# Local attention in a hybrid layer: the values of two chunks multiplied from one tile of weights, with new orders

## The chip, the cores and the metric

One core of one Trainium2 chip. The metric is the device time of one execution in microseconds; the kernel before has a median of 681.46 us over 3 runs (681.15 to 683.61). TensorE is called PE below, VectorE DVE, ScalarE ACT, GpSimd POOL; SP is the queue that issues nearly all DMAs, in its order.

## The reference

A decoder layer in float32 for 2048 tokens of width 1024. One input projection (1024 x 2816) feeds two groups of heads on the same normalised input: chunkwise retention (4 heads) and sliding-window attention (8 query heads, 2 key/value heads, head size 64, window 128). Each group's output is gated by SiLU, both are concatenated, projected back and added to `x`. The attention works in chunks of 128 tokens, each against its own and the preceding 128 keys:

```python
kband, vband = band(k), band(v)          # preceding chunk | this chunk: 256 keys
logits = jnp.einsum('bnqhgd,bnkhd->bhgnqk', qb, kband) * (SWA_HEAD_DIM ** -0.5)
mask = (dist[None] >= 0) & (dist[None] < WINDOW) & (key_pos >= 0)
logits = jnp.where(mask, logits + bias, NEG_INF)
probs = jax.nn.softmax(jnp.concatenate([logits, sink], axis=-1), axis=-1)[..., :-1]
out = jnp.einsum('bhgnqk,bnkhd->bnqhgd', probs, vband)
```

## The kernel before

**Products.** Both projections run as four stages of 2x2 block products with seven multiplications in place of eight (`products`): first 512 columns (attention's q, k, v and half of retention's v), then 384 (retention's q, k and the rest of v), then the gates (512), then the output projection (512). Each float32 operand is split by ACT and DVE into two parts (`split`), and a product is three passes over them. A stage is 7 multiplications x 8 pairs of chunks x 4 x 3 = 672 matmuls on the full array, the `acc<-w,x` of the profile.

**Everything else is fitted between the products.** `Program.emit` is a planner: every operation carries a cost, a due time counted in products and a tile share, and the planner writes one fixed order for each engine. `SHARE` caps the tiles of each use, `AHEAD` and `AHEAD_OF` how early loads may go, `LATER`, `CROWD`, `MOST`, `SOONER` weigh when small matmuls are gathered into one visit, `HELD` lists which intermediate tiles stay on chip instead of going out to DRAM and back, `TURNED` which are transposed by DMA, and `WIN`, `RET`, `GATE`, `LEAD` are due times of the attention, the retention and the gates. Once written, the order is fixed: each engine executes its instructions one after the other. On PE the tiled matmuls of attention and retention stand between runs of products.

**Attention** (`window`, `attend`, `values`). For chunk `c`, `attend` normalises q and k (`qn`, `kn`), turns k on PE (`ident,kn`) and q by DMA (`qT`), and multiplies the logits (`ks,qT`) in bands: each group of 32 queries `u` meets only the 160 keys from `32u` on. DVE adds the bias and takes the maximum, ACT takes the exponential into `lg` (128 x 640 for each key/value head), and a DVE block transpose of 32 x 32 turns `lg` into `pT`. `values` runs once for each pair of chunks. The tile `vn` holds values gathered so that row group `u` (32 partitions) has, in its block `b`, the 32 keys from `32u + 32b` on. The array works as eight tiles of 32 rows x 64 columns (four row groups, two heads). For each chunk of the pair, five blocks are multiplied with 128 columns of `pT` (4 query heads x 32 queries) and accumulated in PSUM; ACT copies the result out (`so`). Block 4 of the first chunk holds the same keys as block 0 of the second.

Tiles of 640 columns (`lg`, `pT`, `vn`) share one pool of nine; `vn` may use three of them.

**Retention** (`retention`) multiplies scores (`qkT`, `state,qkT`), outputs (`v,sT`) and state updates (`v,qk`) between products as well.

Of the kernel before, what the change touches and what calls it, by code (L numbers as in the profile page):

```python
# [29 lines left out]
F32 = mybir.dt.float32  # L30
# [9 lines left out]
P = 128  # L40
NCH = S // P
# [4 lines left out]
GRP = AH // KVH  # L46
# [8 lines left out]

NORMED = 4
SUMMED = 4
CAP = {"k": 84, "h": 6, "wide": 9, "bank": 8}
SMALL, COUNTS = 3, {"ms": 1, "rxt": 1, "rqk0t": 1, "rqk1t": 1}

SHARE = {"x": 18, "raw": 58, "acc": 55, "wr": 20, "wh": 20, "att": 54, "ret": 37, "rin": 49, "gate": 12, "mix": 28, "norm": 5, "res": 6, "turned": 7, "vn": 3, "first": 5, "block": 3, "rest": 6}

AHEAD_OF = {"x": 3.0, "wh": 8.0}

AHEAD, SPARE, SPARED = 13.5, 3, ("raw", "wr")

# [30 lines left out]

LATER, CROWD, MOST, SOONER = 0.0, -0.5, 4, 52.0
SETTLED, INSIDE = 0.8, 0.3


# [33 lines left out]
class Program:  # L139
# [5 lines left out]
    def op(self, cost, go, r=(), w=(), due=0.0, table=None, label="", also=(), many=0):  # L145


        o = Op()
        o.cost, o.go, o.due, o.after, o.set, o.label, o.many = cost, go, due, [], table, label, many * MORE
        o.n, o.left, o.ready, o.end, o.seen, o.by = len(self.ops), 0, 0.0, 0.0, 0.0, None  # L150
        deps = set()
        for b in r:
            if b.writer is not None:
                deps.add(b.writer)
        for b in w:
            if b.writer is not None:
                deps.add(b.writer)
            deps.update(b.readers)
        for b in r:
            b.readers.append(o)  # L160
        for b in w:
            b.writer, b.readers = o, []
        o.bufs = list(dict.fromkeys((*r, *w, *also)))
        for b in o.bufs:
            b.left += 1
        o.new = [b for b in (*w, *also) if b.ap is None and b.tag]
        for d in deps:
            if d is not o:
                d.after.append(o)
                o.left += 1  # L170
        self.ops.append(o)
        return o

    def emit(self):
# [28 lines left out]
        while done < count:  # L203
            best = None
            for e, found in avail.items():
# [4 lines left out]
                for due, n, o in found[:48]:  # L210
# [16 lines left out]
                    for b in o.new:  # L227
                        if b.ap is None:
                            need.setdefault(b.tag, []).append(b)
                    if any(due > now + AHEAD_OF.get(b.share, 1e9) for b in o.new):  # L230
                        continue
# [5 lines left out]
                    for tag, bs in need.items():  # L237
# [7 lines left out]
                        for share in {b.share for b in bs if b.share}:  # L245
                            many = used[share] + sum(b.share == share for b in bs)
                            if many > SHARE[share] - (spare if share in SPARED else 0):
                                short = True
# [90 lines left out]
TURN = (1.9635, 2.7, 1.35)  # L339


HELD = {"sums": ((5, 0), (5, 5), (6, 3), (7, 0), (7, 1), (7, 5), (7, 7)), "ro": (1, 9, 10, 12, 13, 14, 15), "q": (2, 3, 13, 14), "gates": (4, 6, 7), "so": (1, 2, 4, 9, 11)}

TURNED = {"q": range(NCH), "qk": range(NCH), "gated": (0, 2, 6, 8, 11, 13)}
EARLIER_Q, EARLIER_K = -1.0, 9.0
SCALED = (3.0, 2.1)


def dve(n, two=False, lat=0.08):
# [34 lines left out]
def dma(kb, issue=0.45):  # L387
    return {"Q": (0.0315 + kb / 320.95, 2.6, issue)}

VALUES = {"T": (2.28, 2.5, False)}


class Order:
# [27 lines left out]
def layer(ctx, tc, xt, xfirst, xtok, nw, w_in, w_rn, qkw, sinks, biasg, rope, decays, dmask, gpow, w_out, out):  # L423
    nc = tc.nc
    order = Order(tc)
    V, G, A, Q, T = (Engine(order, e) for e in (nc.vector, nc.gpsimd, nc.scalar, nc.sync, nc.tensor))
# [7 lines left out]
    def alloc(b):  # L434
        if b.tag == "bank":
            return psum.tile([P, 512], F32, tag=b.tag, bufs=CAP[b.tag], name=b.name)
        if b.tag in ("k", "h", "wide"):
            n = {"k": 512, "h": 256, "wide": 640}[b.tag]
            return sbuf.tile([P, n], b.dtype, tag=b.tag, bufs=CAP[b.tag], name=b.name)
        return little.tile(b.shape, F32, tag=b.tag, bufs=COUNTS.get(b.tag, SMALL), name=b.name)  # L440

    prog = Program(alloc, {"V": V, "G": G, "A": A, "Q": Q, "T": T})
    op = prog.op
# [5 lines left out]
        return Buf("h", None, F32, name)  # L449

    def wide(name, share=None):
        return Buf("wide", None, F32, name, share)

    def sb(name, shape):
        return Buf(name, shape, F32, name)
# [1 line left out]
    def ps(share="rest", name="m"):  # L457
        return Buf("bank", None, F32, name, share)
# [51 lines left out]
    wr = fixed([P, 4], "wr")  # L510
# [18 lines left out]
    akv_rows = dram.tile([(NCH + 1) * P, 512], F32, name="aq1_dram")  # L529
    akv_dram = {c: Buf(name="aq1_dram", ap=akv_rows[(c + 1) * P : (c + 2) * P, :]) for c in range(-1, NCH)}  # L530
# [139 lines left out]
    def blocks(src, base, seq, keep):  # L670
# [3 lines left out]
        for m, p in seq.all:  # L674
# [6 lines left out]
            elif m == 6:  # L681
# [7 lines left out]
                if keep:  # L689
                    for i, k in enumerate((5, 6, 7, 3)):  # L690
                        if (k, p) in HELD["sums"]:
                            sums[k, p] = held[k, p]
# [5 lines left out]
    sums = {}  # L698
# [50 lines left out]
    turn = Buf(name="turn", ap=())  # L749
# [154 lines left out]
    def retention(at):  # L904
# [18 lines left out]
        for c in range(NCH):  # L923
# [139 lines left out]

            ro = kb("ro", "mix" if c in HELD["ro"] else "ret")
            for i in range(2):
# [20 lines left out]
    def group_norm(st, ros, due):  # L1086
# [26 lines left out]
        for c, ro in ros:  # L1113
# [6 lines left out]
            op({"A": (1.55, 1.65, False)}, go, [ro, rg, nmu], [ro], due + 0.5, label="normalise")  # L1120
            if c in HELD["ro"]:
                held_ro[c] = ro
# [43 lines left out]
    def values(c, held, due):  # L1166


        tiles = []
        for k in range(2):  # L1170

            n = wide("vn", "vn")
            at = akv_rows[(c + k) * P : (c + k + 1) * P, 128:256]
            src = bass.AP(at.tensor, at.offset, [[512, P], [32 * 512, 5], [1, P]])
            op(
                dma(380, 0.6), lambda e, n=n, src=src: e.dma_start(n().rearrange("p (b d) -> p b d", d=P), src),
                [akv_dram[c + k - 1], akv_dram[c + k]], [n], due - 4, label="load vn",
            )
            tiles.append(n)
        pavs = [ps() for _ in range(4)]  # L1180

        def go(e):
            for k, n in enumerate(tiles):
                for b in range(5):
                    for u, q in enumerate(QUARTERS):
                        for g, r in enumerate((L, H)):
                            e.matmul(
                                pavs[u]()[r, k * P : (k + 1) * P].rearrange("p (i s) -> p i s", s=32),
                                n()[q, b * P + g * 64 : b * P + g * 64 + 64],
                                held[k][g]()[q, :].rearrange("p (i b s) -> p i b s", b=5, s=32)[:, :, b, :],  # L1190
                                start=(k == b == 0), stop=(b == 4), skip_group_check=True,
                            )

        op(VALUES, go, tiles + [t for h in held for t in h], pavs, due + 2, "bands", label="values", many=320)
        for k in range(2):
            so = kb("so", "mix" if c + k in HELD["so"] else "att")

            def go(e, so=so, k=k):
                for u in range(4):
                    e.activation(  # L1200
                        so().rearrange("p (i u s) -> p i u s", u=4, s=32)[:, :, u, :],
                        pavs[u]()[:, k * P : (k + 1) * P].rearrange("p (i s) -> p i s", s=32), AF.Copy,
                    )

            op({"A": (0.95, 1.05, False)}, go, pavs, [so], due + 2.1, label="so")
            if c + k in HELD["so"]:
                held_so[c + k] = so
            else:
                store(so_dram[c + k], so, due + 2.2)

    held_q, held_so, sums_of = {}, {}, []

    def qk_sums(p, row, col, b, due):

# [14 lines left out]
        if col == 1:  # L1229
# [4 lines left out]
            )  # L1234
        if col == 0 and c in HELD["q"]:
            held_q[c] = b
# [21 lines left out]
    L, H = slice(0, 64), slice(64, 128)  # L1258
    QUARTERS = [slice(i * 32, i * 32 + 32) for i in range(4)]

    def attend(c, a, b, fac, facs, due, bias_t, ks_t, nsnk):
        slot = c % 2
# [10 lines left out]
        if c in HELD["q"] and c in TURNED["q"]:  # L1273
# [16 lines left out]
            label="turn k", many=2,  # L1290
# [29 lines left out]
        lgs = [wide("lg") for _ in range(KVH)]  # L1320
# [15 lines left out]
        for bank, heads in enumerate([(2 * t + j, g) for j in range(2)] for t in range(2) for g in range(2)):  # L1336
            later, n = due + 0.5 + 0.2 * bank, len(heads)
            pl, g = pls[bank], heads[0][1]
            lg = lgs[g]
            out = Part(lg, lambda t, i=heads[0][0]: t[:, i * 160 : (i + 2) * 160])  # L1340

            part = lambda x, k=bank: x[:, c % SUMMED, k // 2 * 4 + k % 2 : k // 2 * 4 + 4 : 2]
# [4 lines left out]
            def go(e, pl=pl, out=out, heads=heads):  # L1347
# [9 lines left out]
                later, label="bias", also=(nm, lg),  # L1357
            )

            def go(e, out=out, heads=heads):  # L1360
# [9 lines left out]
                also=(nm, den, lg),  # L1370
            )
            weights_of[bank] = out
        pTs = []
        for g in range(KVH):
            lg, pT = lgs[g], wide("pT")
            op(
                {"V": (0.85, 0.95, False)}, lambda e, lg=lg, pT=pT: e.transpose(pT(), lg()), [weights_of[g], weights_of[2 + g]], [pT],
                due + 1.3 + 0.3 * g, label="turn weights", also=(lg,),
            )
            pTs.append(pT)  # L1380
        if c % SUMMED == SUMMED - 1:
# [97 lines left out]
    def go(e):  # L1479
# [10 lines left out]
        label="no values",  # L1490
# [28 lines left out]

WIN = (58.0, 4.8)
RET = (125.0, 2.1)
GATE = (145.0, 5.3)

LEAD = 12.0


_SHAPES = {
# [94 lines left out]
```

## Time and profile before

| | |
|---|---|
| median of 3 runs | 681.46 us (681.15 to 683.61) |
| span of the profiled execution | 679.0 us; the page gives no other time for it |
| PE busy | 672.1 us, 5812 matmuls |
| DVE busy | 594.3 us |
| ACT busy | 462.1 us |
| DMA | 162.63 MB |
| granted clock of PE | 1.000 |

The span runs from the first to the last instruction of the profiled execution. A row of the timeline has start, duration, engine, operation, output and inputs, shapes and count, and in brackets the idle time before it and what ended it. A row of waits has total, times and longest. Matmul ends are modelled, so distances from start to start are safer than durations. A float32 matmul of the program is two matmuls in the trace; a transpose, or a pass of a product, is one.

### The profile page before, as it was taken

The numbers are of one execution on the slowest core, as the hardware profiler recorded it, in microseconds if no ns is written. First come the engines' busy times: TensorE is split into PE (matmuls) and PEld (weight loads), VectorE is DVE, ScalarE is ACT, GpSimd is POOL, SyncE is SP. The second block draws the span as 40 slices with busy tenths as digits, with TensorE's granted clock in tenths as the row PEclk, the third lists the DMA queues.
The fourth block names the chain that finished last, engine by engine and source line by source line (L and its number), as shares of the span: only waits on it lengthen the run. The fifth ranks groups of instructions, "written<-read, shape, count | busy, mean of one in ns | idle before, by whom it ended". The sixth has DMA issues, their size and how long they took to land.

```text
span 679.0 us, 16052 instructions
## 1 busy us (share of the span) xinstructions
PE 672.1 (99%) x5812; PEld 571.4 (84%) x5812; DVE 594.3 (88%) x1369; ACT 462.1 (68%) x1121; POOL 15.6 (2%) x39
## 2 busy tenths in 40 slices
PE   9999999999999999999999999999999999999998
PEld 7888888889998999998878788888888888888886
DVE  6999967788897988999997998998889999997862
ACT  6763897758797776887977588987999844353300
POOL 0000000024100000000000000000000000000000
PEclk9999999999999999999999999999999999999999
DMA  9975698999969879999977879999998986055522
GB/s 314 383 237 217 202 372 291 297 305 296 273 182 248 243 225 280 301 279 319 234 207 246 220 223 288 214 331 253 260 247 219 267 192 199 1 170 171 181 99 94
DMA packets 155439, 162.63 MB, mean 240 GB/s; under 512 B 67808, under 2 KB 96352, under 8 KB 155360
## 3 DMA queue, kind: packets, MB, share of 16 engines
q1 hardware_dynamic: 155216, 161.61, 80.3%
q8 instruction: 46, 0.75, 0.5%
q14 instruction: 33, 0.27, 0.1%
q10 hardware_dynamic: 144, 0.00, 0.0%
HBM read 98.06 MB, written 49.35 MB: 217 GB/s over the span
## 4 chain that ended last, share of the span: by engine, by line
PE 94%; DVE 3%; DMA 2%; issue 1%; ACT 0%; SPq 0%; DVEq 0%; ACTq 0%
PE acc L419 82%; PE m L419 11%; DMA planes_dram<-apart 1%; DMA so_dram<-so 1%; DVE w L419 0%; DVE t L419 0%; DVE x L419 0%; DVE tsin L419 0%; DVE tcos L419 0%; DVE sT L419 0%; DVE state L419 0%; DVE qk L419 0%; ACT c L419 0%; ACT x L419 0%; ACT apart L419 0%
## 5 line engine op out<-in xcount | busy, mean ns | idle before, releaser
L419 PE MATMUL acc<-w,x 128*128 128x512 f32 (+1 forms) x2700 | 591.9, 378 | 0.2 <-PE m L419 0.2
L419 PEld LDWEIGHTS acc<-w,x 128*128 128x128 f32 x2700 | 492.1, 188 | 84.4 <-issue 4.3
L419 DVE TENSOR_TENSOR x<-x 128x512 fp32r<-128x512 f32 (+2 forms) x220 | 145.0, 685 | 17.4 <-ACT x L419 13.6
L419 ACT ACTIVATE x<-x 128x512 fp32r<-128x512 f32 (+1 forms) x187 | 111.8, 616 | 31.7 <-DVE x L419 13.9
L419 DVE TENSOR_TENSOR w<-w 128x512 fp32r<-128x512 f32 (+3 forms) x96 | 62.1, 671 | 3.3 <-ACT w L419 2.4
L419 ACT ACTIVATE lg<-lg,nm 128x160 f32<-128x160 f32 x128 | 53.0, 417 | 11.3 <-DVE nm L419 11.3
L419 DVE TENSOR_TENSOR s<-acc,s 128x512 f32<-128x512 f32 (+1 forms) x64 | 42.3, 660 | 14.5 <-PE acc L419 14.0
L419 DVE SCALAR_TENSOR_TENSOR w<-w,nw_sb 128x512 fp32r<-128x512 f32 (+3 forms) x72 | 49.6, 709 | 1.3 <-ACT w L419 1.3
L419 ACT ACTIVATE w<-w 128x512 fp32r<-128x512 f32 (+1 forms) x72 | 40.7, 603 | 12.8 <-PE acc L419 10.5
L419 DVE CUSTOM_DVE_ANT_0 lg<-m,bias,nsnk 128x160 f32<-128x160 f32 x128 | 40.6, 383 | 2.4 <-PE m L419 2.3
L419 DVE TENSOR_TENSOR t<-acc,t 128x512 f32<-128x512 f32 (+2 forms) x33 | 21.1, 641 | 15.0 <-PE acc L419 14.9
L419 ACT ACTIVATE s<-acc 128x512 f32<-128x512 f32 (+1 forms) x32 | 18.2, 569 | 17.3 <-PE acc L419 13.2
L419 ACT ACTIVATE w<-w,nw_sb 128x512 fp32r<-128x512 f32 (+3 forms) x43 | 27.6, 677 | 2.7 <-DMA w<-in_w_in 2.7
L419 DVE TENSOR_TENSOR r<-acc,t 128x512 f32<-128x512 f32 (+1 forms) x32 | 21.0, 655 | 9.1 <-PE acc L419 8.5
L419 ACT ACTIVATE x<-go 128x512 fp32r<-128x512 f32 x25 | 15.5, 626 | 17.6 <-PE acc L419 7.9
L419 ACT ACTIVATE ro<-ro,nmu,rg 128x128 f32<-128x128 f32 x64 | 25.1, 481 | 2.8 <-DVE nmu L419 2.8
L419 DVE STREAM_TRANSPOSE pT<-lg 128x640 f32<-128x640 f32 x32 | 25.7, 831 | 0.9 <-ACT lg L419 0.9
L419 DVE TENSOR_TENSOR t<-acc,s 128x512 f32<-128x512 f32 (+1 forms) x32 | 21.4, 667 | 4.8 <-PE acc L419 2.9
L419 ACT ACTIVATE apart<-qn 128x1024 uint16<-128x1024 uint16 x16 | 16.8, 1057 | 11.0 <-DVE qn L419 10.8
L419 ACT ACTIVATION_READ_ACCUMULATOR lg<-lg,nm 128x1 f32 x128 | 24.2, 189 | 0.0
L419 PE MATMUL m<-pT,vn 32*64 32x128 f32 x1280 | 21.2, 273 | 1.2 <-issue 0.8
L419 PE MATMUL m<-ks,qT 64*32 64x160 f32 x1024 | 22.1, 300 | 0.1
(144 smaller groups left out, 598.4 us busy)
## 6 DMA issues: line engine op xcount, KB each, us to landing
x<-in_xt SPq DMA_DIRECT2D x80, 256.0 KB, 4.7
planes_dram<-apart SPq DMA_DIRECT2D x54, 256.0 KB, 3.6
x<-s_dram SPq DMA_DIRECT2D x50, 256.0 KB, 4.3
w<-in_w_in SPq DMA_DIRECT2D x40, 256.0 KB, 5.1
xk<-in_xtok SPq DMA_DIRECT2D x32, 256.0 KB, 5.0
res<-in_xtok SPq DMA_DIRECT2D x32, 256.0 KB, 3.7
s_dram<-x SPq DMA_DIRECT2D x25, 256.0 KB, 3.9
vn<-aq_dram SPq DMA_DIRECT2D x16, 320.0 KB, 5.1
```

Source lines behind the costliest of these rows:

```text
L419: return lambda *a, **k: self.order.put(op(*a, **k))
```

## The change

Both chunks of a pair now use one `vn` of nine blocks (128 x 1152, 576 KB, one DMA). Block `b` below 4 is multiplied with the first chunk's columns, above 4 with the second's, and the shared block 4 once, with 256 columns that run over both chunks. For that, `pT` of both chunks of a pair lie in one tile of 1280 columns for each key/value head. The pool of nine becomes three pools: `lg` three tiles, `pT` two, `vn` one. The planner's cost for `values`, its instruction count (320 to 288) and its other settings are new, so all orders are planned anew.

```diff
-CAP = {"k": 84, "h": 6, "wide": 9, "bank": 8}
+CAP = {"k": 84, "h": 6, "lg": 3, "pT": 2, "vn": 1, "bank": 8}
-SHARE = {"x": 18, "raw": 58, "acc": 55, "wr": 20, "wh": 20, "att": 54, "ret": 37, "rin": 49, "gate": 12, "mix": 28, "norm": 5, "res": 6, "turned": 7, "vn": 3, "first": 5, "block": 3, "rest": 6}
-AHEAD_OF = {"x": 3.0, "wh": 8.0}
-AHEAD, SPARE, SPARED = 13.5, 3, ("raw", "wr")
+SHARE = {"x": 29, "raw": 58, "acc": 56, "wr": 22, "wh": 20, "att": 47, "ret": 22, "rin": 41, "gate": 9, "mix": 29, "norm": 7, "res": 24, "turned": 8, "vn": 3, "first": 5, "block": 3, "rest": 6}
+AHEAD_OF = {"x": 2.5, "wh": 6.5}
+AHEAD, SPARE, SPARED = 14.5, 4, ("raw", "wr")
-LATER, CROWD, MOST, SOONER = 0.0, -0.5, 4, 52.0
+LATER, CROWD, MOST, SOONER = 1.75, -1.0, 1, 32.0
-HELD = {"sums": ((5, 0), (5, 5), (6, 3), (7, 0), (7, 1), (7, 5), (7, 7)), "ro": (1, 9, 10, 12, 13, 14, 15), "q": (2, 3, 13, 14), "gates": (4, 6, 7), "so": (1, 2, 4, 9, 11)}
+HELD = {"sums": ((5, 0), (5, 5), (6, 4), (6, 6), (7, 1), (7, 2)), "ro": (1, 5, 8, 11, 12, 13, 15), "q": (3, 13, 14), "gates": (4, 5), "so": (0, 3, 6, 7, 11, 13)}
-TURNED = {"q": range(NCH), "qk": range(NCH), "gated": (0, 2, 6, 8, 11, 13)}
-EARLIER_Q, EARLIER_K = -1.0, 9.0
-SCALED = (3.0, 2.1)
+TURNED = {"q": range(NCH), "qk": range(NCH), "gated": (0, 2, 6, 7, 14, 15)}
+EARLIER_Q, EARLIER_K = 0.5, 9.0
+SCALED = (0.0, 2.35)
-VALUES = {"T": (2.28, 2.5, False)}
+VALUES = {"T": (2.05, 2.27, False)}
...
     def values(c, held, due):
-        tiles = []
-        for k in range(2):
-            n = wide("vn", "vn")
-            at = akv_rows[(c + k) * P : (c + k + 1) * P, 128:256]
-            src = bass.AP(at.tensor, at.offset, [[512, P], [32 * 512, 5], [1, P]])
...
-        pavs = [ps() for _ in range(4)]
+        n = wide("vn")
+        at = akv_rows[c * P : (c + 1) * P, 128:256]
+        src = bass.AP(at.tensor, at.offset, [[512, P], [32 * 512, 9], [1, P]])
...
+        pavs, pTs = [ps() for _ in range(4)], [t.whole for t in held[0]]
         def go(e):
-            for k, n in enumerate(tiles):
-                for b in range(5):
-                    for u, q in enumerate(QUARTERS):
-                        for g, r in enumerate((L, H)):
-                            e.matmul(
-                                pavs[u]()[r, k * P : (k + 1) * P].rearrange("p (i s) -> p i s", s=32),
-                                n()[q, b * P + g * 64 : b * P + g * 64 + 64],
-                                held[k][g]()[q, :].rearrange("p (i b s) -> p i b s", b=5, s=32)[:, :, b, :],
-                                start=(k == b == 0), stop=(b == 4), skip_group_check=True,
-                            )
-        op(VALUES, go, tiles + [t for h in held for t in h], pavs, due + 2, "bands", label="values", many=320)
+            for b in range(9):
+                for u, q in enumerate(QUARTERS):
+                    for g, r in enumerate((L, H)):
+                        t = pTs[g]()[q, :].rearrange("p (i b s) -> p i b s", b=5, s=32)
+                        k = b // 5
+                        if b == 4:
+                            x = t[:, 0:4, 4, :]
+                            part, x = pavs[u]()[r, 0 : 2 * P], bass.AP(x.tensor, x.offset, [x.ap[0], [512, 2], [160, GRP], [1, 32]])
+                            part = part.rearrange("p (k i s) -> p k i s", k=2, s=32)
+                        else:
+                            part, x = pavs[u]()[r, k * P : (k + 1) * P].rearrange("p (i s) -> p i s", s=32), t[:, 4 * k : 4 * k + 4, b - 4 * k, :]
+                        e.matmul(
+                            part, n()[q, b * P + g * 64 : b * P + g * 64 + 64], x, start=(b == 0), stop=(b in (4, 8)),
+                            skip_group_check=True,
+                        )
+        op(VALUES, go, [n, *(t for h in held for t in h)], pavs, due + 2, "bands", label="values", also=pTs, many=288)
...
-            lg, pT = lgs[g], wide("pT")
+            if slot == 0:
+                wholes[g] = wide("pT")
+            lg, pT = lgs[g], Part(wholes[g], lambda t: t[:, slot * 640 : slot * 640 + 640])
...
-WIN = (58.0, 4.8)
-RET = (125.0, 2.1)
-GATE = (145.0, 5.3)
-LEAD = 12.0
+WIN = (56.0, 4.8)
+RET = (124.5, 2.1)
+GATE = (143.0, 5.5)
+LEAD = 13.5
```

More of the change, by code (lines that the diff above doesn't have):

```diff
@@ L436, in alloc @@
             return psum.tile([P, 512], F32, tag=b.tag, bufs=CAP[b.tag], name=b.name)
-        if b.tag in ("k", "h", "wide"):
-            n = {"k": 512, "h": 256, "wide": 640}[b.tag]
+        if b.tag in ("k", "h", "lg", "pT", "vn"):
+            n = {"k": 512, "h": 256, "lg": 640, "pT": 1280, "vn": 1152}[b.tag]
             return sbuf.tile([P, n], b.dtype, tag=b.tag, bufs=CAP[b.tag], name=b.name)
@@ L451, in wide @@
     def wide(name, share=None):
-        return Buf("wide", None, F32, name, share)
+        return Buf(name, None, F32, name, share)
     def sb(name, shape):
@@ L1166, in values @@
     def values(c, held, due):
-        tiles = []
-        for k in range(2):
-            n = wide("vn", "vn")
-            at = akv_rows[(c + k) * P : (c + k + 1) * P, 128:256]
-            src = bass.AP(at.tensor, at.offset, [[512, P], [32 * 512, 5], [1, P]])
-            op(
-                dma(380, 0.6), lambda e, n=n, src=src: e.dma_start(n().rearrange("p (b d) -> p b d", d=P), src),
-                [akv_dram[c + k - 1], akv_dram[c + k]], [n], due - 4, label="load vn",
-            )
-            tiles.append(n)
@@ L1180, in values @@
-        pavs = [ps() for _ in range(4)]
-        def go(e):
-            for k, n in enumerate(tiles):
-                for b in range(5):
-                    for u, q in enumerate(QUARTERS):
-                        for g, r in enumerate((L, H)):
-                            e.matmul(
-                                pavs[u]()[r, k * P : (k + 1) * P].rearrange("p (i s) -> p i s", s=32),
-                                n()[q, b * P + g * 64 : b * P + g * 64 + 64],
-                                held[k][g]()[q, :].rearrange("p (i b s) -> p i b s", b=5, s=32)[:, :, b, :],
-                                start=(k == b == 0), stop=(b == 4), skip_group_check=True,
-                            )
@@ L1194, in values @@
-        op(VALUES, go, tiles + [t for h in held for t in h], pavs, due + 2, "bands", label="values", many=320)
+        n = wide("vn")
+        at = akv_rows[c * P : (c + 1) * P, 128:256]
+        src = bass.AP(at.tensor, at.offset, [[512, P], [32 * 512, 9], [1, P]])
+        op(
+            dma(580, 0.6), lambda e: e.dma_start(n().rearrange("p (b d) -> p b d", d=P), src),
+            [akv_dram[c + k] for k in (-1, 0, 1)], [n], due - 4, label="load vn",
+        )
+        pavs, pTs = [ps() for _ in range(4)], [t.whole for t in held[0]]
@@ new lines, in go @@
+        def go(e):
+            for b in range(9):
[12 more added lines that the diff above has]
+                            skip_group_check=True,
+                        )
@@ L1209, in values @@
                 store(so_dram[c + k], so, due + 2.2)
-    held_q, held_so, sums_of = {}, {}, []
+    held_q, held_so, sums_of, wholes = {}, {}, [], {}
     def qk_sums(p, row, col, b, due):
@@ L1374, in attend @@
         for g in range(KVH):
-            lg, pT = lgs[g], wide("pT")
+            if slot == 0:
+                wholes[g] = wide("pT")
+            lg, pT = lgs[g], Part(wholes[g], lambda t: t[:, slot * 640 : slot * 640 + 640])
             op(
                 {"V": (0.85, 0.95, False)}, lambda e, lg=lg, pT=pT: e.transpose(pT(), lg()), [weights_of[g], weights_of[2 + g]], [pT],
-                due + 1.3 + 0.3 * g, label="turn weights", also=(lg,),
+                due + 1.3 + 0.3 * g, label="turn weights", also=(lg, wholes[g]),
             )
```

## Prediction

> **What bounds the kernel now.** I read the page first, then the waits of TensorE (PE), the busy time by stretches, and PE's timeline around the bursts that the change touches.
>
> ```profile
> span 679.0 us, 16052 instructions
> PE 672.1 (99%) x5812; PEld 571.4 (84%) x5812; DVE 594.3 (88%) x1369; ACT 462.1 (68%) x1121; POOL 15.6 (2%) x39
> ...
> PE 94%; DVE 3%; DMA 2%; issue 1%; ACT 0%; SPq 0%; DVEq 0%; ACTq 0%
> ```
> ```profile
> PE m L419 <- DVE none L419: 1.2, 1, 1.2
> PE m L419 <- issue: 0.8, 1, 0.8
> PE m L419 <- ACT c L419: 0.5, 1, 0.5
> PE m L419 <- DVE state L419: 0.4, 1, 0.4
> PE m L419 <- DVE sT L419: 0.4, 1, 0.4
> ```
> ```profile
> 20.00:140.00 120.00, 120.00 (x531) 99.38 (x530) 105.69 (x195) 82.99 (x187) 0.00 (x0) 1.00 0.83 285
> ...
> 164.00:400.00 236.00, 233.87 (x3463) 207.42 (x3462) 212.55 (x601) 180.96 (x557) 6.97 (x13) 1.00 0.90 250
> 400.00:542.00 142.00, 141.58 (x1037) 117.58 (x1036) 131.78 (x329) 124.98 (x245) 0.00 (x0) 1.00 0.95 260
> ```
>
> PE is busy 672.1 of 679.0 us and carries 94% of the chain of waits. Its waits (second fence: total, times, longest) are 1.2 us at the start and 0.8 + 0.5 + 0.4 + 0.4 = 2.1 us in all that follows. The stretches give per engine busy time and count, then the granted clock (1.00 throughout) and the DMA share: in the attention and retention stages DVE is at 90 and 93%, DMA at 90 and 95%, both below PE. So the end is set by the amount and packing of PE's work. A change gains by taking work or mode changes off PE, and loses by making PE wait. The page gives the profiled execution no time beside its span. The 681.46 us median stands 2.5 us above the span, and I carry that difference over unchanged.
>
> **Part 1: the values burst.** Per pair of chunks, 160 hardware matmuls (80 calls, two each for float32) become 144 (72 calls). Eight tiles of 32 rows by 64 columns work at once.
>
> ```profile
> 186.23 4.43 PE L419 MATMUL acc<-w,x 128*128 128x384 f32 x24
> 190.59 1.34 PE L419 MATMUL m<-ks,qT 64*32 64x160 f32 x64
> 191.86 1.84 PE L419 MATMUL acc<-w,x 128*128 128x384 f32 x9
> 193.63 2.56 PE L419 MATMUL m<-pT,vn 32*64 32x128 f32 x160
> 196.12 4.96 PE L419 MATMUL acc<-w,x 128*128 128x384 f32 x27
> ...
> 204.99 7.56 PE L419 MATMUL acc<-w,x 128*128 128x384 f32 x42
> 212.48 2.09 PE L419 MATMUL m<-pT,vn 32*64 32x128 f32 x129
> 215.33 0.69 PE L419 MATMUL m<-pT,vn 32*64 32x128 f32 x31 [0.76 <-issue]
> 215.95 0.80 PE L419 MATMUL acc<-w,x 128*128 128x384 f32 x3
> ```
> ```profile
> 441.03 0.67 PE L419 MATMUL m<-qkT 64*64 64x128 f32 x16
> 441.52 0.62 PE L419 MATMUL m<-state,qkT 64*64 64x128 f32 x16
> 442.06 3.06 PE L419 MATMUL acc<-w,x 128*128 128x512 f32 x12
> ...
> 456.88 0.67 PE L419 MATMUL m<-qkT 64*64 64x128 f32 x16
> ...
> 457.80 0.62 PE L419 MATMUL m<-qkT 64*64 64x128 f32 x16
> ...
> 458.67 0.62 PE L419 MATMUL m<-qkT 64*64 64x128 f32 x16
> 459.11 0.62 PE L419 MATMUL m<-state,qkT 64*64 64x128 f32 x16
> 459.66 0.98 PE L419 MATMUL acc<-w,x 128*128 128x512 f32 x3
> ```
>
> I take times from start to next start, since the ends are modelled. An undisturbed values burst takes 196.12 - 193.63 = 2.49 us. What of that is streaming, the retention scores tell: three chunks take 459.66 - 456.88 = 2.78 us, one takes 442.06 - 441.03 = 1.03, so a chunk adds (2.78 - 1.03) / 2 = 0.875. It has 32 matmuls on four tiles, eight rounds, so one round of 128 float32 columns takes 0.109 us, and 1.03 - 0.875 = 0.155 is the cost of the mode. Values have 160 / 8 = 20 rounds: 2.19, with the mode 2.34. Of the 2.49 only 0.15 is neither.
>
> After the change a burst has 16 rounds of 128 columns and 2 of 256, which are again 20 rounds' worth: **the shared block is multiplied in fewer instructions, not in fewer columns.** So at most the 0.15 can go, if fewer instructions keep the tiles better fed. I take two thirds, 0.10 us, eight times: **-0.8 us**. The upper end is a burst that is bound by its instruction count: a tenth of 2.49, 0.25 each, -2.0. The lower end is below zero: the trace has no tiled matmul of 256 columns, and a long row could run slower than two short ones. The nearest rows:
>
> ```profile
> 1.18 3.78 PE L419 MATMUL m<-none 128*128 128x256 f32 x8 [1.18 <-DVE none L419]
> 4.86 2.53 PE L419 MATMUL acc<-w,x 128*128 128x512 f32 x7
> ```
>
> There eight float32 matmuls of 256 columns took 4.86 - 1.18 = 3.68 us, 0.46 each, against 2 x 0.109 = 0.218 here. At that pace two rounds would cost 2 x (0.46 - 0.218) = 0.48 more per burst, +3.9 us in all. I don't take it: they are the program's first matmuls, and the products' longer rows of 512 columns hold 120 / 531 = 0.226 us without any penalty. It stays in the range.
>
> [...]
>
> **Part 2: the order on PE.** Counted in the two built orders, PE leaves the full-array products for tiled matmuls 33 times before and 30 times after, and changes the tiling inside such a visit 7 times before and 10 after (half the logits now often stand directly behind the values). A visit costs 0.155 inside (above), and the run of products beside it also loses: 18 products more (42 against 24) take 7.49 - 4.36 = 3.13 us, 0.174 each, so the run of 24 lost 4.36 - 24 x 0.174 = 0.18 at its ends. Together 0.34. A change of tiling inside a visit spares the products, so I give it 0.155. Three visits fewer and three changes more: -1.02 + 0.47 = **-0.6 us** (between -1.0, if the change of tiling is free, and 0, if it costs like a visit). Products, logits, scores, updates, outputs and transposes are the same in number.
>
> **Part 3: what is moved or newly waits.** The 16 loads of 320 KB for `vn` become 8 of 576 KB; and the pools shrink to one `vn` tile, two `pT` tiles that hold both chunks, and three `lg`.
>
> ```profile
> vn<-aq_dram SPq DMA_DIRECT2D x16, 320.0 KB, 5.1
> ...
> q8 instruction: 46, 0.75, 0.5%
> ```
> ```profile
> SPq L419 <- PE acc L419: 54.4, 60, 5.8
> L419 DVE STREAM_TRANSPOSE pT<-lg 128x640 f32<-128x640 f32 x32 | 25.7, 831 | 0.9 <-ACT lg L419 0.9
> ```
>
> With one tile, the load for a pair can be issued only when the previous pair's matmuls are done. Bursts stand 212.48 - 193.63 = 18.9 us apart in the closest rows. The load, by size 576 / 320 x 5.1 = 9.2 us as an upper estimate, leaves 18.9 - 2.5 - 9.2 = 7 us: hidden, as long as SP gets to it. If not, PE waits in the burst and every product queued behind waits too. The two `pT` tiles are rewritten (0.83 us on DVE each) only after logits that stand behind the values on PE anyway: nothing. The new hand-picked lists move other traffic. Counted in the orders: five transfers of 256 KB more (query, gate and sum spills, less one output spill), eight `vn` loads fewer, so 0.77 MB more, 3.1 us at the 250 GB/s of the stretch 164 to 400. DMA is free there for 236 x 0.10 + 142 x 0.05 = 31 us over the two stretches, so it is covered; uncovered it costs those 3 us. DVE and ACT keep their numbers of operations.
>
> **Part 4: the stalls.** Three of the pauses in the trace:
>
> ```profile
> 354.94 0.46 PE L419 MATMUL m<-pT,vn 32*64 32x128 f32 x12
> 355.83 2.40 PE L419 MATMUL m<-pT,vn 32*64 32x128 f32 x148 [0.43 <-DVE state L419]
> ...
> 367.06 0.38 PE L419 MATMUL m<-qkT 64*64 64x128 f32 x2
> 367.93 0.55 PE L419 MATMUL m<-qkT 64*64 64x128 f32 x11 [0.50 <-ACT c L419]
> ```
>
> The burst at 212.48 took 215.95 - 212.48 = 3.47 us instead of 2.49, with a pause that waits for nothing shown ("issue"). I read it as instructions arriving late: queue 8 brought 46 pieces for PE's 2 x 5812 instructions, some 253 each, and a values burst alone is 320. [...] After the change a burst is 288, so such pauses get a little rarer, but where they fall depends on where a piece ends, which the new order moves everywhere. The new plan will have its own late operands too. I leave the 2.1 us of waits as they are: 0, between -2.1 and several us more.
>
> **Sum:** -0.8 - 0.6 + 0 + 0 = -1.4 us, 681.46 - 1.4 = **680.1 us**. A measurement of this kernel can tell some 0.5%, 3.4 us, from no change: below 678.05 is faster, above 684.87 slower.
>
> **Rivals.** *Instructions are the bound (faster).* If bursts are paced by instruction count, they give -2.0, the visits -0.6, and with thinner bursts and more lookahead (`AHEAD` 13.5 to 14.5, more `x` tiles) the 2.1 us of waits go: -4.7, 676.8 us. For it: the "issue" pause. Against it: the 109 ns rounds, and that all three must come together; the instructions and visits alone end at 678.9, inside "same". [...]
>
> *One `vn` tile holds up SP's queue (slower).* SP issues in order. Where the `vn` load waits for the values, the query turns, spills and the `x` loads of the next products wait behind it. SP's waits on products come to 54.4 us in 60, 0.9 each, and the longest is 5.8. If each of the seven loads that must wait delays the products by one such mean wait, 7 x 0.9 = 6.3: 680.1 + 6.3 = 686.4 us. It decides once SP is held longer than the loads behind it are early. For it: DMA at 90 to 95% leaves late loads little room to catch up. Against it: the 7 us of slack, and that PE barely waited with SP waiting this often.
>
> *The change does not shorten the burst at all* (only columns count): -0.6, 680.9 us, inside "same"; with slow 256-column rows 680.9 + 3.9 = 684.8, just inside it.
>
> **How the numbers follow.** Forecast with its neighbours inside 0.5% (also the burst unshortened): 0.47. Faster: 0.28, as removing mode changes and instructions is the sure part and the stalls that could go are there to see. Slower: 0.25, since late operands have no upper bound while the gain has one. The range runs from below the faster rival (676.8, less the bound of -1.0 for the visits in place of -0.6: 676.4) to the slower rival, 686.4; what lies outside is deep stalls above and a saving nobody in these rows explains below, at most 2 in 10.
>
> **What would show it.** Right: a values burst of 2.3 to 2.45 us from start to next start; 144 matmuls in it, 16 of them with 256 columns; PE above 98% busy; waits of PE after the start still 1 to 4 us; eight `vn` loads, none with PE waiting on it. Wrong towards faster: bursts near 2.25. Wrong towards slower: PE idle before `acc` or `m` with a DMA, `x` or `pT` named, longer SP waits on `m`, or bursts above 2.6 us without a pause in them.

## The result, and the profile after

The changed kernel is slower: 685.33 us (20 runs, 683.25 to 692.92) against 681.31 us (20 runs, 679.36 to 685.41), a ratio of 1.0076 with a 95% interval of 1.0058 to 1.0095. The forecast was 680.1 us and most likely no measurable change; the direction was wrong, and by the forecast's own bar of 684.87 the kernel is slower. The range held the time. The profiled execution took 684.4 us with a span of 682.6.

The page and the waits of PE of the changed kernel (total, times, longest):

```profile
span 682.6 us, 15825 instructions
PE 671.4 (98%) x5684; PEld 570.3 (84%) x5684; DVE 594.9 (87%) x1370; ACT 463.8 (68%) x1122; POOL 16.1 (2%) x39
PE 81%; DMA 6%; DVE 5%; ACT 5%; issue 2%; SPq 0%; ACTq 0%; DVEq 0%
```
```profile
PE m L419 <- issue: 1.5, 1, 1.5
PE acc L419 <- ACT s L419: 1.4, 1, 1.4
PE m L419 <- DVE s L419: 1.3, 1, 1.3
PE acc L419 <- DVE x L419: 1.2, 1, 1.2
PE m L419 <- DVE none L419: 1.2, 1, 1.2
PE m L419 <- DVE state L419: 0.5, 1, 0.5
PE m L419 <- DVE t L419: 0.4, 1, 0.4
PE m L419 <- DVE sT L419: 0.3, 1, 0.3
```

PE waits 6.6 us after the start where the kernel before waited 2.3 (all its rows summed; the prediction left out the smallest). Four waits of 1.2 to 1.5 us make up most of it, and PE's share of the chain falls from 94 to 81%. PE is also busy 0.7 us less than before (671.4 us), but its work did not become smaller. The 0.7 us lie in the first 12 us, shown here for the kernel before and the changed one:

```profile
4.86 7.53 PE L419 MATMUL acc<-w,x 128*128 128x512 f32 x29
4.79 7.58 PE L419 MATMUL acc<-w,x 128*128 128x512 f32 x32
```

The changed kernel starts three products more, 3 x 0.226 = 0.7 us: the first products of the kernel before stand some 0.43 us apart up to 6.3 us, those of the changed one 0.23 us almost at once. By the starts of single products, from the 41st product on (14.72 and 14.02 us) to PE's last matmul (675.79 and 679.27 us), less the waits, PE works 658.8 us before and 658.7 after. So the span's +3.6 us are the waits' +4.3 less the 0.7 of the start, and nothing is left over for the work.

The values bursts on PE's timeline, the first and the third:

```profile
188.01 2.53 PE L419 MATMUL m<-pT,vn 32*64 32x128 f32 x144
190.47 0.80 PE L419 MATMUL acc<-w,x 128*128 128x384 f32 x3
...
238.71 2.48 PE L419 MATMUL m<-pT,vn 32*64 32x128 f32 x138
242.64 0.44 PE L419 MATMUL m<-pT,vn 32*64 32x128 f32 x6 [1.45 <-issue]
243.01 0.78 PE L419 MATMUL m<-ks,qT 64*32 64x160 f32 x32
243.72 4.43 PE L419 MATMUL acc<-w,x 128*128 128x384 f32 x24
248.08 0.77 PE L419 MATMUL m<-ks,qT 64*32 64x160 f32 x32
248.79 1.50 PE L419 MATMUL acc<-w,x 128*128 128x384 f32 x7
```

An undisturbed burst takes 190.47 - 188.01 = 2.46 us, where the kernel before took 2.49 in its first burst and, by the starts of its single matmuls, 2.466 in others. Sixteen matmuls and sixteen weight loads fewer gained 5 ns. The third burst stands still 1.45 us for instructions. Half the logits directly behind it take 0.71 us (243.01 to 243.72).

Two of the late operands, on the timeline of ACT, DVE and PE:

```profile
162.57 0.49 ACT L419 ACTIVATE s<-acc 128x384 f32<-128x384 f32 x1 [1.73 <-DMA aq_dram<-t]
163.12 1.14 PE L419 MATMUL acc<-w,x 128*128 128x384 f32 x5 [1.38 <-ACT s L419]
...
348.09 0.37 DVE L419 CUSTOM_DVE_ANT_0 lg<-m,bias,nsnk 128x160 f32<-128x160 f32 x1
348.40 0.37 DVE L419 CUSTOM_DVE_ANT_0 lg<-m,bias,nsnk 128x160 f32<-128x160 f32 x1
348.70 0.68 DVE L419 TENSOR_TENSOR x<-x 128x512 fp32r<-128x512 f32 x1
349.43 0.73 PE L419 MATMUL acc<-w,x 128*128 128x512 f32 x2 [1.21 <-DVE x L419]
```

At 163.1 a product waits for the copy of its PSUM bank, and that copy waits for an output transfer (`aq_dram<-t`) to land. At 349.4 a product waits for its `x`, which stands on DVE behind the biases of a chunk's logits. Neither has to do with the values burst; both are places in the new order.

### The profile page after: what moved, and what is told of

It is laid out like the page before. It is cut to its first block, busy times and chain, and to the rows that moved or that the text cites. A ratio compares the mean times of both kernels' runs of the same rounds, so it can differ in the third digit from the quotient of the medians.

```text
span 682.6 us, 15825 instructions
## 1 busy us (share of the span) xinstructions
PE 671.4 (98%) x5684; PEld 570.3 (84%) x5684; DVE 594.9 (87%) x1370; ACT 463.8 (68%) x1122; POOL 16.1 (2%) x39
## 4 chain that ended last, share of the span: by engine, by line
PE 81%; DMA 6%; DVE 5%; ACT 5%; issue 2%; SPq 0%; ACTq 0%; DVEq 0%
PE acc L419 71%; PE m L419 11%; DMA aq_dram<-t 2%; DMA planes_dram<-apart 2%; DMA w<-in_w_in 1%; DVE x L419 1%; ACT x L419 1%; ACT sq L419 1%; DVE s L419 1%; ACT apart L419 1%; ACT qk L419 1%; DVE w L419 1%; DMA aq_dram<-r 1%; ACT lg L419 0%; SPq L419 0%
## 5 line engine op out<-in xcount | busy, mean ns | idle before, releaser
L419 ACT ACTIVATE so<-m 128x128 f32<-128x128 f32 x64 | 11.9, 294 | 17.2 <-PE m L419 10.2
L419 PE MATMUL m<-pT,vn 32*64 32x128 f32 (+1 forms) x1152 | 21.1, 285 | 1.5 <-issue 1.5
```

The lines of the kernel that those rows point to most:

```text
L419: return lambda *a, **k: self.order.put(op(*a, **k))
```

## The experiments

**Columns or instructions: the burst by itself.** First, the orders of the changed kernel left as they are, with the shared block multiplied twice with 128 columns again.

```diff
-            for b in range(9):
+            for b, k in [(b, 0) for b in range(5)] + [(b, 1) for b in range(4, 9)]:
...
```

> The changed kernel with its orders on every engine unchanged, but the shared block multiplied twice with 128 columns again (160 matmuls per burst for 144). Theory A (columns set the burst, orders set the loss): the burst stays at 2.46 to 2.47 us from start to next start, and the time stays with the changed kernel's, 685.3 us give or take 1.5. Rival B (instructions set the burst): 16 matmuls more cost 0.25 us per burst, 2.71, and 687.3 us. Rival C (the rows of 256 columns or their addressing are what made it slower): the 4 us come back, 681.3.

Then with the second half of the shared block left out.

```diff
                         if b == 4:
                             x = t[:, 0:4, 4, :]
-                            part, x = pavs[u]()[r, 0 : 2 * P], bass.AP(x.tensor, x.offset, [x.ap[0], [512, 2], [160, GRP], [1, 32]])
-                            part = part.rearrange("p (k i s) -> p k i s", k=2, s=32)
+                            part = pavs[u]()[r, 0:P].rearrange("p (i s) -> p i s", s=32)
```

> The changed kernel with the second half of the shared block left out: block 4 is multiplied with the first chunk's 128 columns alone, 144 matmuls per burst as before and two half rounds fewer. Theory A (columns set the burst): 2.46 - 2 x 0.109 = 2.24 us from start to next start. Rival B (instructions set the burst): 2.46 as in the changed kernel.

PE's timeline, first of the doubled block, then of the halved one:

```profile
291.01 2.54 PE L419 MATMUL m<-pT,vn 32*64 32x128 f32 x160
293.48 0.75 PE L419 MATMUL m<-ks,qT 64*32 64x160 f32 x26
297.13 0.47 PE L419 MATMUL m<-ks,qT 64*32 64x160 f32 x6 [2.90 <-issue]
297.53 6.52 PE L419 MATMUL acc<-w,x 128*128 128x384 f32 x27
```
```profile
269.67 2.32 PE L419 MATMUL m<-pT,vn 32*64 32x128 f32 x144
271.92 0.77 PE L419 MATMUL m<-ks,qT 64*32 64x160 f32 x32
```

With 160 matmuls the burst takes 293.48 - 291.01 = 2.47 us, with 144 and two half rounds less 271.92 - 269.67 = 2.25: 0.21 less than the changed kernel's 2.46, near the expected 2 x 0.109. **The burst is set by its columns.** The one time of the halved kernel, 685.88 us, tells nothing beyond that: its waits are 8.7 us.

The time of the doubled block was a miss for every theory: 694.45 us (ratio 1.016, 1.0112 to 1.0209), though the order on every engine is the same. Its trace names the reason in the fence above: pauses for instructions, 7.2 us in three on the matmuls `m` alone. PE's instructions come in packets of queue 8, a piece of 256 in each: in the traces of the kernel before and of the changed one 11504 and 11247 of them (matmuls, weight loads and semaphore instructions) start between the first packet and the last, 255.6 for each packet. With 256 more on PE (16081 instructions in all against 15825) the page counts 46 packets in place of 45, and the pieces end at other places of the same order; that three ends now fall on dense bursts is the author's reading of the three pauses. And a pause costs more than itself: the busy time by stretches around the pause at 294 to 297 (after the engines' busy times: granted clock, DMA share and rate; the third row is a part of the second),

```profile
294.00:297.40 3.40, 0.50 (x16) 0.14 (x5) 0.51 (x1) 1.44 (x7) 0.00 (x0) 1.00 0.96 255
297.40:303.00 5.60, 5.60 (x28) 5.47 (x23) 3.46 (x12) 4.94 (x14) 0.00 (x0) 0.70 0.40 143
298.10:301.50 3.40, 3.40 (x13) 3.40 (x12) 2.00 (x8) 3.40 (x12) 0.00 (x0) 0.50 0.44 157
303.00:309.00 6.00, 6.00 (x65) 5.46 (x63) 6.00 (x18) 3.11 (x11) 0.00 (x0) 1.00 0.83 250
```

shows the granted clock at 0.50 for 3.4 us behind it, in which the products start 0.32 us apart in place of 0.17. The trace has such stretches at three places, 13.7 us in all, which at half the clock cost up to 6.8 us. With the waits' 5.5 us over the changed kernel's they cover the span's 10.3. The pause is 2.90 us by the row; other runs show the same behind shorter ones (last section).

**Code or settings.** First the new values code and its pools with the settings of the kernel before (`SHARE`, `AHEAD_OF`, `AHEAD`, `LATER`, `HELD`, `TURNED`, `EARLIER_Q`, `SCALED`, `VALUES`, `WIN`, `RET`, `GATE`, `LEAD` and what stands on their lines), some of them here against the changed kernel:

```diff
-AHEAD, SPARE, SPARED = 14.5, 4, ("raw", "wr")
+AHEAD, SPARE, SPARED = 13.5, 3, ("raw", "wr")
...
-LATER, CROWD, MOST, SOONER = 1.75, -1.0, 1, 32.0
+LATER, CROWD, MOST, SOONER = 0.0, -0.5, 4, 52.0
...
-WIN = (56.0, 4.8)
-RET = (124.5, 2.1)
-GATE = (143.0, 5.5)
+WIN = (58.0, 4.8)
+RET = (125.0, 2.1)
+GATE = (145.0, 5.3)
```

> The new values code and the new pools (lg three, pT two, vn one) with all of the planner's settings of the kernel before (tile shares, lookahead, held tiles, due times) and its cost for values. Theory A (the new settings' orders bring late operands): waits of PE back near 3 us, 680 to 683 us. Rival C (the values code or its small pools cost the time): 684 to 687 us. Rival D (any new order is a draw, whatever the settings): anything from 679 to 690, with stalls at new places.

Then the reverse: the kernel before, its code and pools untouched, with those settings of the changed kernel, except that `VALUES` stays at 2.28.

```diff
-AHEAD, SPARE, SPARED = 13.5, 3, ("raw", "wr")
+AHEAD, SPARE, SPARED = 14.5, 4, ("raw", "wr")
...
-WIN = (58.0, 4.8)
-RET = (125.0, 2.1)
-GATE = (145.0, 5.3)
+WIN = (56.0, 4.8)
+RET = (124.5, 2.1)
+GATE = (143.0, 5.5)
```

> The values code and the pool of the kernel before, with all of the planner's settings of the changed kernel. Theory A (the new settings' orders bring late operands): 684 to 687 us. Rival C (the values code or its small pools cost the time): 680 to 682 us. Rival D (any new order is a draw): anything from 679 to 690, and the stalls not at the places where the changed kernel has them.

Measured: 698.68 us (1.0249, 1.0202 to 1.0296) and 691.62 us (1.0129, 1.0093 to 1.0165). Both halves of the change by themselves are slower than the whole. That fits neither A nor C, and both times lie above D's range (679 to 690) too. What is left is D's mechanism, worse than expected: new orders stall at new places. That settings and code belong together, because the settings were picked for the order they give, is the reading that the runs below test. Among PE's waits with the old settings

```profile
PE acc L419 <- ACT w L419: 4.6, 2, 3.3
PE acc L419 <- DVE w L419: 3.7, 2, 1.9
PE m L419 <- DVE sT L419: 2.8, 3, 1.4
```

the first two are weights, which the changed kernel never waited for.

**Instructions that arrive late.** The orders untouched, only the stream of PE's instructions shifted at the start: most warming matmuls are replaced by many of one column, 23 in the changed kernel (shown) and 34 in the kernel before.

```diff
-        for _ in range(WARM):
+        for _ in range(2):
             e.matmul(pw()[:, 0:256], none()[:, 0:P], none()[:, 0:256], start=True, stop=True)
+        for _ in range(23):
+            e.matmul(pw()[0:1, 256:257], none()[:, 0:1], none()[:, 0:1], start=True, stop=True)
```

> The changed kernel with its orders unchanged; only its instructions on TensorE stand 84 places later (two of the four warm-up calls at the start give way to 23 multiplications of one column), so that its pieces of 256 instructions end at other places. Theory A (pauses in a burst are instructions arriving late, the other long waits are late operands): the pause of 1.6 us in the burst at 238.7 is gone, the waits on ACT s (1.4), DVE x (1.2), DVE s (1.3) stay at their places, and the time falls by 1 to 2 us to 683 to 684.5. Rival (the pause is a late operand or a bank that the profile doesn't show): it stays, 685.3. Should a pause come up at another burst instead, A holds too, but without a gain.

> The kernel before with its orders unchanged and its instructions on TensorE 128 places later (two warm-up calls give way to 34 multiplications of one column). [...] Rival (where the pieces end doesn't matter): 681.3.

PE's timeline in the changed kernel shifted, at the third burst, and in the kernel before shifted:

```profile
243.97 2.53 PE L419 MATMUL m<-pT,vn 32*64 32x128 f32 x144
246.43 0.78 PE L419 MATMUL m<-ks,qT 64*32 64x160 f32 x32
```
```profile
266.52 2.27 PE L419 MATMUL m<-pT,vn 32*64 32x128 f32 x139
271.79 0.66 PE L419 MATMUL m<-pT,vn 32*64 32x128 f32 x21 [3.00 <-issue]
272.37 0.33 PE L419 MATMUL m<-ident,kn 128*128 128x128 f32 x1
```

In the first the pause is gone (246.43 - 243.97 = 2.46), and in the second a burst without a pause before got one of 3.00 us: 688.28 us (1.0114, 1.0081 to 1.0147), 7.0 us above the 681.3 expected should it not matter where the pieces end. (Of the 2.3 us of waits in the kernel before, one of 0.8 was for instructions.)

But the edit does a second thing: it takes away half of the warming. The first 12 us of the kernel before shifted and of the changed kernel shifted:

```profile
4.96 7.25 PE L419 MATMUL acc<-w,x 128*128 128x512 f32 x20
4.62 7.61 PE L419 MATMUL acc<-w,x 128*128 128x512 f32 x21
```

They start 20 products where the kernel before starts 29, and 21 for the changed kernel's 32. At the 41st product that is 1.85 and 2.35 us lost. So of the 7.4 us of span that the kernel before lost by the shift, some 5.5 are left for the places where the pieces end: pauses for instructions of 5.7 us in place of 0.8, and a stretch at half the clock behind the longest. The pieces themselves are packets of queue 8 in the traces. In all 14 pauses above 0.3 us that the traces of these runs put down to "issue", PE goes on 1.2 to 1.6 us after such a packet has landed (at 270.21 and 271.79 us for the pause of 3.00). That instructions arrive late is shown.

The changed kernel came to 684.41 us (1.0066, 1.0028 to 1.0105); the expected gain of 1 to 2 us over 685.33 cannot be told from none. Its start lost 2.35 us, and the wait on `ACT s` takes 2.88 us in place of 1.38, with the granted clock at 0.50 for 3.4 us behind it. Not all late operands stayed either: the wait on `DVE x` takes 0.5, that on `DVE s` is gone, and one of 1.4 on `DVE state` before a product is new. So these waits change with the time at which PE comes to them, at an unchanged order.

**A draw, or the planner's cost.** `VALUES` tells the planner what a burst costs. The change lowered it by a tenth with the instruction count, from 2.28 to 2.05; the burst stayed the same, so the new plan counts on 0.23 us per burst that never came. Four kernels try this. The kernel before with one due time moved by 0.1:

```diff
-WIN = (58.0, 4.8)
+WIN = (58.1, 4.8)
```

> The kernel before with one due time of the attention moved by 0.1 (WIN 58.0 to 58.1), and the orders planned anew from it. Theory D (any new order is a draw, and the kernel before is a good one): 683 to 692 us, with stalls of TensorE above 1.5 us at places where the kernel before has none. Rival (orders from nearly the same settings run nearly alike): 680 to 682.5.

The changed kernel with the cost put back:

```diff
-VALUES = {"T": (2.05, 2.27, False)}
+VALUES = {"T": (2.28, 2.5, False)}
```

> The changed kernel with the planner's cost for the values put back to that of the kernel before (2.28 for 2.05), which is what a burst of 2.46 us corresponds to, and planned anew. Theory E (the planner was misled by a cost that is 0.23 us too small per burst): operand waits shrink, 681 to 683.5. Theory D (any new order is a draw, and the settings were picked for the order that they gave): 684 to 695.

The changed kernel with the due time moved, and then with both edits:

```diff
-WIN = (56.0, 4.8)
+WIN = (56.1, 4.8)
```

> The changed kernel with one due time of the attention moved by 0.1 (WIN 56.0 to 56.1), planned anew. Theory D (an order picked with its settings, and any new one is a draw): slower than the changed kernel by several us, 688 to 698, with waits of 1.5 us or more at new places. Rival (the settings set the loss): within 2 us of the changed kernel, 683 to 687.

> The changed kernel with the cost of the values put back to 2.28 and the same due time moved by 0.1, planned anew. Theory E (the cost that was too small is what made the changed kernel slower, and putting it right brings it back): 681 to 684 once more. Theory D (the good result with the cost put right was itself a draw): 684 to 692.

And two orders for the new code with the cost at 2.27, picked out of many drawn from small changes of the settings. Against the changed kernel, the first has

```diff
-SHARE = {"x": 29, "raw": 58, "acc": 56, "wr": 22, "wh": 20, "att": 47, "ret": 22, "rin": 41, "gate": 9, "mix": 29, "norm": 7, "res": 24, "turned": 8, "vn": 3, "first": 5, "block": 3, "rest": 6}
+SHARE = {'x': 29, 'raw': 58, 'acc': 56, 'wr': 23, 'wh': 20, 'att': 47, 'ret': 22, 'rin': 41, 'gate': 9, 'mix': 29, 'norm': 7, 'res': 27, 'turned': 7, 'vn': 3, 'first': 5, 'block': 3, 'rest': 6}
-AHEAD_OF = {"x": 2.5, "wh": 6.5}
+AHEAD_OF = {'x': 2.61, 'wh': 6.5}
-LATER, CROWD, MOST, SOONER = 1.75, -1.0, 1, 32.0
+LATER, CROWD, MOST, SOONER = 0.66, -0.55, 2, 41.6
-VALUES = {"T": (2.05, 2.27, False)}
+VALUES = {"T": (2.27, 2.5, False)}
-WIN = (56.0, 4.8)
-RET = (124.5, 2.1)
-GATE = (143.0, 5.5)
+WIN = (57.4, 4.841)
+RET = (125.26, 2.044)
+GATE = (143.04, 5.472)
-LEAD = 13.5
+LEAD = 12.27
```

> The changed kernel's values code with its cost set to 2.27, as measured, and the order picked out of some 1700 drawn by small changes of due times, tile shares and lookahead. Theory D (orders are draws, and a good one is found by drawing; the values code itself is worth nothing either way): 678 to 682 us, like the kernel before, the bursts still 2.46 us, waits of PE after the start at most 3 us. Rival C (the values code or its pools cost the time): not below 684.

and the second

```diff
-AHEAD_OF = {"x": 2.5, "wh": 6.5}
+AHEAD_OF = {'x': 2.5, 'wh': 7.02}
-AHEAD, SPARE, SPARED = 14.5, 4, ("raw", "wr")
+AHEAD, SPARE, SPARED = 14.82, 4, ('raw', 'wr')
-LATER, CROWD, MOST, SOONER = 1.75, -1.0, 1, 32.0
+LATER, CROWD, MOST, SOONER = 1.03, -0.59, 1, 32.6
-SCALED = (0.0, 2.35)
+SCALED = (-0.61, 2.349)
-VALUES = {"T": (2.05, 2.27, False)}
+VALUES = {"T": (2.27, 2.5, False)}
-WIN = (56.0, 4.8)
-RET = (124.5, 2.1)
-GATE = (143.0, 5.5)
+WIN = (58.53, 4.738)
+RET = (124.57, 1.969)
+GATE = (142.34, 5.565)
```

> As the run before it, from a second and independent series of draws, which ended at other settings. Theory D: 678 to 682 us, with what waits there are at other places than in the first. Rival C: not below 684.

All kernels in one table; the waits are the sum of PE's waits after the start in the profiled execution, the span and PE's mean granted clock are that execution's. Each ratio is against the runs of the kernel before beside that kernel, and need not be the quotient of two medians of the table.

| kernel | median us | ratio to before (95%) | span us | PE waits us | clock |
|---|---|---|---|---|---|
| before | 681.31 | | 679.0 | 2.3 | 1.000 |
| changed | 685.33 | 1.0076 (1.0058 to 1.0095) | 682.6 | 6.6 | 1.000 |
| before_nudged | 691.37 | 1.0163 (1.0125 to 1.0202) | 689.0 | 11.0 | 0.993 |
| after_nudged | 696.68 | 1.0220 (1.0184 to 1.0255) | 695.6 | 11.3 | 0.995 |
| true_cost | 682.52 | 1.0022 (0.9999 to 1.0045) | 679.0 | 3.6 | 1.000 |
| true_cost_nudged | 684.84 | 1.0056 (1.0034 to 1.0079) | 683.2 | 5.7 | 1.000 |
| replanned_1 | 680.57 | 0.9982 (0.9963 to 1.0002) | 675.4 | 1.4 | 1.000 |
| replanned_2 | 678.00 | 0.9951 (0.9931 to 0.9971) | 675.8 | 1.8 | 0.999 |
| old_settings | 698.68 | 1.0249 (1.0202 to 1.0296) | 697.1 | 14.9 | 0.988 |
| new_settings | 691.62 | 1.0129 (1.0093 to 1.0165) | 690.5 | 9.1 | 0.995 |
| before_shifted | 688.28 | 1.0114 (1.0081 to 1.0147) | 686.4 | 6.6 | 0.997 |
| after_shifted | 684.41 | 1.0066 (1.0028 to 1.0105) | 683.8 | 5.1 | 0.997 |
| shared_twice | 694.45 | 1.0160 (1.0112 to 1.0209) | 692.9 | 12.1 | 0.990 |

Spans and waits rise together, from 675.4 us with 1.4 to 697.1 with 14.9. The span rises by more, 21.7 us for 13.5, and where it does the clock is lower: behind long waits it stands at 0.50 for 3.4 us or several times that. A due time moved by 0.1 made the kernel before 10 us slower. The two largest waits of that kernel are for weights of the last stage that come late:

```profile
PE acc L419 <- DVE w L419: 5.0, 2, 4.4
PE acc L419 <- ACT w L419: 2.9, 1, 2.9
PE acc L419 <- ACT x L419: 1.4, 2, 0.8
```

So orders from nearly equal settings lie 2 to 11 us apart: shown, in three pairs. All three moved due times came out slower than what they were moved from, as settings would that were picked for their order. And the new code with its pools is no handicap: replanned_2, whose orders hold one `vn` tile, two `pT` and three `lg`, beats the kernel before by 0.5%. That is no gain of the new code: its order was picked out of many, and no such search for the code before is among the runs. Its page and its waits:

```profile
span 675.8 us, 15824 instructions
PE 669.4 (99%) x5684; PEld 571.3 (85%) x5684; DVE 594.2 (88%) x1370; ACT 462.0 (68%) x1120; POOL 16.9 (3%) x39
...
PE m L419 <- DVE none L419: 1.2, 1, 1.2
PE m L419 <- DVE sT L419: 0.9, 1, 0.9
PE acc L419 <- ACT s L419: 0.9, 2, 0.6
```

Its undisturbed bursts are still 2.46 us; its gain over the changed kernel is 2.0 us less busy time of PE, whose source is not shown, and 4.8 us less waiting. The true cost was the better one in both pairs (682.52 against 685.33, 684.84 against 696.68), but the first time lies in theory E's range and the second in D's. Two pairs, in draws that scatter by 10 us, do not settle whether the false cost caused the changed kernel's waits. That stays open.

## Why the prediction was wrong

- **The bound** was right: every kernel here ends by PE's work plus PE's waits. Missing was that PE's work takes longer behind a long wait (products 0.32 us apart in place of 0.17 for 3.4 us, shared_twice), and that its start varies: 0.7 us in favour of the changed kernel.
- **The values burst (-0.8 us)** was mis-sized: 0.03 us against the kernel before's first burst, 5 ns against its others, in place of 0.10 each (a forecast of 2.3 to 2.45 us, measured 2.46). The argument (20 rounds' worth of columns before and after) was right, and a burst not shortened at all stood among the rivals; taking two thirds of the 0.15 us that were "neither" had no row behind it. The slow rows of 256 columns (+3.9 us) did not come either: the eight matmuls that spoke for them stand at the start, where the products behind them were slow too (0.43 us apart). Eight bursts with 16 matmuls fewer each brought 8 x 5 ns = 0.04 us.
- **The visits (-0.6 us)** do not show: behind the start, PE's work is the same in both traces (658.8 and 658.7 us). One price held: half the logits behind a burst takes 0.71 us twice, 1.42, against 1.27 for the whole set before (190.59 to 191.86), 0.15 for the split, as estimated. What took the rest back stays open.
- **The one `vn` tile** held up nothing that the trace shows: no wait of PE names a `vn` load, and replanned_2 has the same pool. SP's waits on `m` did grow, as this rival said (13.9 us before), while those on `acc` fell from 54.4 to 45.5:

```profile
SPq L419 <- PE m L419: 24.4, 26, 3.8
```

- **The stalls (0)** are the step that failed. The text said "I leave the 2.1 us of waits as they are: 0, between -2.1 and several us more". With the wait that it left out these were 2.3 us, and they became 6.6: +4.3 where the sum had 0, more than the whole +3.6 of the span. The text saw that the new plan has late operands of its own, but kept the middle at 0, as if the order before were typical. It is not: the nearest order to it that was run waits 11.0 us. Against draws like these a new order starts with several us to lose and 2.3 us of waits to gain, and the chances (0.28 faster, 0.25 slower) should have leaned to slower. The slower case was there with its size (686.4 us), but with another mechanism, so that the range held the time is luck.

## What to carry to other kernels

When a bound engine's order is written out ahead, the order is itself a tuned object: price a change that plans it anew by the scatter of orders from nearly equal settings, measured on one or two of them, before pricing the instructions it saves. Count what streams, not what is issued: here merging two tiled multiplications into one of twice the columns left the burst at 2.46 us (2.47 with 16 matmuls more), and two half rounds of columns fewer took 0.21 us off it. And when a planner's cost is changed along with an edit, measure the new cost first; here it was scaled by the instruction count while the time stayed.

## What the runs showed of the hardware that was not expected

A long pause of PE is paid again: behind the 2.90 us above, the granted clock stood at 0.50 for 3.4 us, which cost up to 1.7 us more. Every pause of 2.37 us and more in the traces of these runs was followed by such a stretch, ran into one or lay in one. Of seven pauses of 1.97 to 2.18 us, four were followed by one and three were not; the changed kernel's four, of at most 1.45 us, were not. The changed kernel's runs fit this in part: the six with a mean clock of 1.000 took 683.25 to 685.03 us, the four at 0.995 or less 689.01 to 692.92, but those between spread from 683.36 to 691.37.

One-column multiplications did not warm PE as the wide ones do. With two of the four warming calls replaced by 23 or 34 of one column, the trace's first record of the full clock stands at 10.1 and 10.2 us; in the twelve kernels with all four it stands at 4.4 to 6.9 us. Until then the first products stand some 0.43 us apart, afterwards 0.23.

Code loading came to some 5.5 us at an unchanged order on every engine (before_shifted), through the places where pieces of 256 instructions end (255.6 to a packet, as counted above). PE went on 1.2 to 1.6 us after the packet had landed; why a packet comes late is not shown.
